# A hybrid decoder layer in split fp32: branch low parts on one engine, output weights staged in twos, and four PSUM banks for the first output tiles

## The chip, the cores and the metric

The kernel runs on one core of one Trainium2 chip. The core has five engines, each with its own list of instructions that it works through in order: PE (TensorE, matrix products, with PEld for its weight loads), DVE (VectorE), ACT (ScalarE), POOL (GpSimd) and SP (SyncE, which here only issues DMAs). The engines wait for one another through semaphores. PE reads its operands from SBUF and writes its products to PSUM. The metric is the device time of one execution in microseconds.

## The reference

One pre-norm decoder layer (DEPTH is 1) with 1024 positions and model width 1024, in fp32:

```python
h = rmsnorm(x, norm_mix)
dq, dk, dv, rq, rk, rv, rg, lx, ly, gates = jnp.split(h @ w_in, splits, axis=-1)
od  = diff_attention(dq, dk, dv, lam)           # then rmsnorm
o_r = silu(rg) * group_norm_heads(retention_chunkwise(q_r, k_r, v_r, log_g))
o_l = rg_lru_branch(lx, ...) * gelu(ly)
g = sigmoid(gates.reshape(bn, s_len, 3, 1024))
merged = (g[:, :, 0] * (od @ w_branch[0]) + g[:, :, 1] * (o_r @ w_branch[1])
          + g[:, :, 2] * (o_l @ w_branch[2]))
x = x + merged @ w_out
x = x + cross_attention(rmsnorm(x, norm_xattn), rmsnorm(mem, norm_mem)) @ xa_wo
x = x + square(relu(rmsnorm(x, norm_mlp) @ mlp_w1)) @ mlp_w2
return rmsnorm(x, norm_final)
```

The change lies at `merged` and at `merged @ w_out`.

## The kernel before

*Split products.* Every fp32 operand of a product is held as two parts: a high part, which ACT makes by a cast (`dst.hi`, L70), and a low part, the rest, which DVE or POOL makes by a subtraction (`dst.lo`, L71; the third argument of `split` chooses the engine). A product is three matmuls: high by high, high by low, low by high (`mm3`, L59 to L61). A 128x512 unit of weights and a 128x1024 piece of an activation block are split in this way before PE can use them.

*The branch products.* The three products `o @ w_branch` are computed transposed, with seven half-size products in place of eight (a Strassen-Winograd scheme). A *pair* is two 128-column strips of a branch's weights. For each of the seven products k of a pair, `product` (L1161) accumulates four `mm3`, twelve matmuls, in one PSUM bank; DVE adds the results into the temporaries `t0` and `t1` (L1182, L1184, L1187), and when an output quarter is complete it calls `emit`. The order of k in a pair is `ORDER = (1, 2, 6, 7, 5, 4, 3)`, in the last two pairs `LAST = (1, 2, 6, 7, 5, 3, 4)`. A branch has four pairs: 0 and 1 run one after the other, 2 and 3 alternate product by product.

*Weights of a pair.* `h_products` makes a list of preparations, `prep(p, k)`, and each product takes the next one from it (`ahead`), so that a unit is prepared some products before its use. `prepare` (L1140) splits the weight unit of (p, k). Low parts of k = 1 and 2 go to DVE; those of the others to the engine that `prep` (L669) passes: POOL for the pairs before number m, which belong to the input projections, and for the branches (p >= m) DVE where k is 6 or 4 and POOL where k is 7, 5 or 3. After k = 2, `left` (L1117) lets DVE make the sums of weight quarters. `pair_load` loads the raw weights into a staging buffer; its L1128 is the DMA.

*Activation blocks.* Seven blocks of 128x(4x512) hold the right operands of a branch. `fill_block` (L787) issues the two DMAs of one block and then splits the block of the call before. The blocks of the next branch are loaded during the last two pairs of the one that runs. Blocks live in two pools of four slots, `slotA` and `slotB`.

*emit* (in `branch`, L819): load the gate tile `sgb` (five buffers), sigmoid on ACT, load the partial sum of the branches before (`pv`), then on DVE `o = x + y` (L828), `o *= sg` (L829), `o += pv` (L831), and a store to DRAM (L833). In the third branch the upper half of the result (n >= 4) is not stored but split straight into the blocks `mT[j][1]` (L835); the lower half is stored and loaded again as `mT[j][0]` by `fill_block` (L867 to L871).

*The end of the third branch.* The weights of the output product, `w_o`, come in eight units of 128x1024; the first four (the left 512 output columns) pass through one staging tile `wst` of 128x(2x512) and are split into two blocks of `slotB`, at k = 7, 5, 3 and 4, by DVE and POOL in turn (L872 to L880). The load of the next unit is issued right behind each split. A last `fill_block()` (L881) splits `mT[0][0]`. The other four units (right columns) are loaded and split by `weight` (L83), low parts on POOL.

*The output product*, `w_out` (L884): for each pair of 128-row tiles and each column half `cb` two PSUM banks of the pool `ps` (which has two in all) accumulate eight `mm3` each. The first half of the rows uses `mT[1]`, the second `mT[0]`. DVE adds the product to the rows of x (L906); for `cb == 1` the row is stored and normed, and its transposes are put off by one step (`later`). The pool `xps` has room for the cross-attention's tiles `tp`, `sc` and `av`; nothing uses `sc` while `w_out` runs.

*What sets the order.* The code above is emitted in program order, and the framework's scheduler turns it into one list per engine at build time. It goes by program order as priority and by its own estimates of when operands and buffers come free, so later work can stand among earlier work where it expects a gap. `after(key, ins)` keeps instructions with the same key in program order: `hdma` the block and `wst` loads, `wdma` the weight loads, `wsplit` the casts of weights. On the chip each list is worked through strictly in that order.

Of the kernel before, what the change touches and what calls it, by code (L numbers as in the profile page):

```python
# [9 lines left out]
F32 = mybir.dt.float32  # L10
# [7 lines left out]
P = 128  # L18
S = 1024
D = 1024  # L20
KT = 8
HB = 512
MEM = 256
# [26 lines left out]
class Kernel:  # L50
# [596 lines left out]
    def h_products(self):  # L647


        nc, v, a = self.nc, self.nc.vector, self.a  # L650
# [17 lines left out]

        def prep(p, k):  # L669
            self.pair_load(p, *pairs[p])  # L670
            self.prepare(k, pairs[p][0], v if p >= m and k in (6, 4) else nc.gpsimd)

            turns = [x for x in (0, m - 2, m + 2, m + 6, m + 10) if x <= p < x + 2]
            q, at = (p + 1, 6) if not turns else (turns[0] + 2, 3 if p > 1 else 4)
            if k == at and p == (turns or [p])[0] and q < len(pairs):
                self.pair_load(q, *pairs[q])
# [135 lines left out]
    def branch(self, order, i, right, bw, sps, nxt):  # L812

        nc, v = self.nc, self.nc.vector
        after, load = (None, None) if nxt is None else self.load_blocks(nxt)
        mT = [[None, None], [None, None]]
        cs = self.bcs[order]

        def emit(n, j, x, y):  # L819
            rows, sl = slice(n * P, (n + 1) * P), slice(j * HB, (j + 1) * HB)  # L820
            sg = bw.tile([P, HB], F32, tag="sg", name="sgb", bufs=5)
            nc.sync.dma_start(sg, self.gsp[i * D + n * P:i * D + (n + 1) * P, sl])
            nc.scalar.activation(sg, sg, AF.Sigmoid)
            if order > 0:
                pv = bw.tile([P, HB], F32, tag="pv", name="pv", bufs=3)
                nc.sync.dma_start(pv, self.acc[order - 1][rows, sl])
            o = bw.tile([P, HB], F32, tag="y", name="y", bufs=4)
            v.tensor_tensor(o, x, y, op=ALU.add)  # L828
            v.tensor_tensor(o, o, sg, op=ALU.mult)  # L829
            if order > 0:  # L830
                v.tensor_tensor(o, o, pv, op=ALU.add)  # L831
            if nxt is not None or n < 4:
                nc.sync.dma_start(self.acc[order][rows, sl], o)  # L833
            else:
                self.split(mT[j][1][:, n % 4, :], o)  # L835

        def run(p, k):
            self.ahead()
            self.product(k, cs[p], right, self.p6(sps), lambda e, j, x, y: emit(2 * p + e, j, x, y))

        for p in range(2):
            for k in self.ORDER:
                run(p, k)

                if (p, k) == (0, 1):
                    next(self.loading)
                elif (p, k) == (0, 2):
                    self.fill_block()
        if nxt is not None:
            for at, k in enumerate(self.ORDER):  # L850
                run(2, k)
                if at > 0:
                    next(load)
                run(3, k)
            self.loading = load
            return after
        w, units = [], 0
        for k in self.LAST:
            run(2, k)
            run(3, k)  # L860

            if k == 1:
                mT[0][1] = self.block(self.slotA)
            elif k == 6:
                mT[1][1] = self.block(self.slotB)
            elif k in (2, 3):
                j = 3 - k  # L867
                mT[j][0] = self.block(self.slotA)
                x = self.acc[2][:, j * HB:(j + 1) * HB].rearrange("(k p) c -> p k c", p=P)
                self.fill_block(mT[j][0], x)  # L870

            if k in (7, 5, 3, 4):  # L872
                if k in (7, 3):
                    w.append(self.block(self.slotB))
                q = units % 2
                self.split(w[-1][:, 2 * q:2 * q + 2, :], wst, (v, nc.gpsimd)[q])
                units += 1
            if k in (1, 7, 5, 3):
                wst = bw.tile([P, 2, HB], F32, tag="wst", name="wst")
                self.after("hdma", nc.sync.dma_start(wst, self.a["w_o"][0, units].rearrange("p (k c) -> p k c", k=2)))  # L880
        self.fill_block()  # L881
        return mT, w

    def w_out(self, half, mT, w, hx, work, psum):  # L884

        nc, a = self.nc, self.a
        for jp in (0, 2):
            xts = []
            for cb in range(2):
                pss = [self.ps.tile([P, HB], F32, tag="mm", name="pso") for _ in range(2)]  # L890

                for kt, e in [(kt, e) for q in range(2) for e in range(2) for kt in range(4 * q, 4 * q + 4)]:
                    s = slice((jp + e) * P, (jp + e + 1) * P)
                    self.mm3(pss[e], mT[1 - half][kt // 4][:, kt % 4, s], w[cb][kt // 2][:, kt % 2, :], kt == 0, kt == KT - 1)
                for e in range(2):
                    j = jp + e
                    rows, back = (slice((4 * n + j) * P, (4 * n + j + 1) * P) for n in (half, 1 - half))
                    if cb == 0:
                        xts.append(work.tile([P, D], F32, tag="xt", name="xt2", bufs=2))
                        (nc.sync if half or jp else nc.scalar).dma_start(xts[e], a["x"][back, :])  # L900
                        if half == 0 and j == 0:
                            self.gx = self.gain(work, 1)
                    xt = xts[e]
                    ps = pss[e]
                    sl = slice(cb * HB, (cb + 1) * HB)
                    nc.vector.tensor_tensor(xt[:, sl], xt[:, sl], ps, op=ALU.add)  # L906
                    if cb == 1:
                        nc.sync.dma_start(self.x2[rows, :], xt)
                        xs = self.norm_rows(xt, self.gx, work)
                        self.later(lambda xs=xs, j=j: self.rows_T(xs, [b[:, :, j * P:(j + 1) * P] for b in hx], psum))  # L910
# [440 lines left out]
    def run(self):  # L1351
        tc, nc, a = self.tc, self.nc, self.a
        pool = lambda name, bufs=1, side="right", **kw: tc.tile_pool(name=name, bufs=bufs, side=side, reuse_waits="tile", **kw)
        self.setup()
        with pool("slotA", bufs=4, side="left") as self.slotA:
            self.n_gates, self.gate_order = 0, [b * 8 + n for b in (1, 0, 2) for n in range(8)]
            with pool("ret") as self.rp, pool("rps", space=PSUM) as self.rps:
                self.retention(pool)
            with pool("att") as self.ap, pool("aps", space=PSUM) as self.aps:
                self.attention()  # L1360
            with pool("slotB", bufs=4) as self.slotB:
                with pool("sps", space=PSUM) as sps:
                    with pool("sp") as self.sp:
                        self.sps = sps
                        for _ in self.hp:
                            pass
                    with pool("bw") as bw:
                        right = self.branch(0, 1, self.right, bw, sps, 0)
                        right = self.branch(1, 0, right, bw, sps, 2)
                        mT, w0 = self.branch(2, 2, right, bw, sps, None)  # L1370
                A, B = self.slotA, self.slotB
                with pool("work") as work:
                    with pool("xps", bufs=2, space=PSUM) as xps:
                        w = [[w0[u // 2][:, u % 2 * 2:u % 2 * 2 + 2, :] for u in range(4)]]
                        w.append([self.weight(a["w_o"][1, u], 2) for u in range(4)])
                        hx = [[self.block(s) for s in (B, A)]]
                        self.w_out(0, mT, w, hx[0], work, xps)
                        hx.append([self.block(s) for s in (A, B)])
                        self.w_out(1, mT, w, hx[1], work, xps)
                        self.mem_slot()  # L1380
                        self.mem_norm(work)
                        g = self.xattn(hx, work, xps)
                    with pool("mps", space=PSUM) as self.mps:
                        self.xa_last(g)
                        self.mlp_in()
                    with pool("m2ps", bufs=6, space=PSUM) as m2ps:
                        self.mlp_out(m2ps)
# [76 lines left out]
```

## Time and profile before

| what | value |
|---|---|
| three runs | 2419.88, 2423.28, 2424.56 us (median 2423.28) |
| the profiled execution, its own time | 2424.15 us |
| its span on the core | 2422.4 us, mean granted PE clock 0.981 |
| busy PE / PEld | 2319.7 / 1913.1 us |
| busy DVE / ACT / POOL | 1888.0 / 1041.4 / 955.9 us |

The three branches run from about 1240 to 1498 us after the span's start, and the output product from 1498 to 1614. A row of the profile's groups names the source line, the engine, the operation and the tiles (out<-in); then the count, the busy time and the mean duration in ns, and the idle time of the engine just before those instructions with what ended most of it. A timeline row begins with the start and the duration in us, and where the engine stood idle before, the idle time and its releaser stand in brackets. `SPq` and `ACTq` are the sequencers that issue DMAs. A row of the windows view gives the stretch and its length, and then for PE, PEld, DVE, ACT and POOL the busy time with the count of instructions, and at the end the granted clock, the DMA share and GB/s. A row of the waits view gives the total, the number of waits and the longest.

### The profile page before, as it was taken

How to read it: one execution, taken by the hardware profiler on the slowest of the kernel's cores; microseconds unless marked ns; L12 is line 12 of the kernel's file. 1: busy time of each engine (PE TensorE's matmuls, PEld its weight loads, DVE VectorE, ACT ScalarE, POOL GpSimd, SP SyncE). 2: the span in 40 equal slices, each digit the busy share in tenths (PEclk: the TensorE clock that was granted, in tenths of full speed). 3: DMA queues.
4: the chain of work that ended last, by engine and by line, in shares of the span. 5: the costliest groups of instructions: out<-in, count | busy, mean ns of one | idle time of the engine just before them, and what ended most of it. 6: DMA issues, size and time to landing. Idle time of an engine off the chain costs nothing. (4 is left out here: it accounts for less than half of the span.)

```text
span 2422.4 us, 31108 instructions
## 1 busy us (share of the span) xinstructions
PE 2319.7 (96%) x11156; PEld 1913.1 (79%) x11156; DVE 1888.0 (78%) x2909; ACT 1041.4 (43%) x1817; POOL 955.9 (39%) x621
## 2 busy tenths in 40 slices
PE   9999999999999998999999988999989999899998
PEld 7888878888887876777887767778768888788886
DVE  7677487878797788798787898344788888788896
ACT  5443355555555543554354444135442222343333
POOL 1122212222215444455431223034155555598863
PEclk9999999999999999999999999999999999999999
DMA  5222122222215354543576687343225443744341
GB/s 173 81 87 70 58 70 60 64 71 70 62 49 180 127 162 162 174 134 136 178 266 240 228 287 239 105 146 119 97 83 183 152 144 135 254 167 166 121 165 70
DMA packets 135994, 335.12 MB, mean 138 GB/s; under 512 B 17040, under 2 KB 27281, under 8 KB 135840
## 3 DMA queue, kind: packets, MB, share of 16 engines
q1 hardware_dynamic: 135264, 331.30, 41.4%
q8 instruction: 89, 1.46, 0.2%
q10 hardware_dynamic: 576, 1.84, 0.2%
q14 instruction: 65, 0.53, 0.1%
HBM read 227.64 MB, written 97.05 MB: 134 GB/s over the span
## 5 line engine op out<-in xcount | busy, mean ns | idle before, releaser
L59 PE MATMUL ps<-block,wu 128*128 128x512 f32 x1428 | 568.6, 398 | 27.2 <-DVE sf L1187 10.4
L61 PE MATMUL ps<-block,wu 128*128 128x512 f32 x1428 | 565.3, 396 | 10.2 <-DVE wu L71 10.2
L60 PE MATMUL ps<-block,wu 128*128 128x512 f32 x1428 | 561.9, 394 | 0.8 <-DVE block L71 0.8
L71 POOL TENSOR_TENSOR wu<-st,wu 128x512 fp32r<-128x512 f32 x144 | 227.3, 1585 | 303.4 <-ACT wu L70 290.4
L59 PEld LDWEIGHTS ps<-block,wu 128*128 128x128 f32 x1428 | 272.4, 191 | 89.0 <-DVE sf L1187 11.3
L61 PEld LDWEIGHTS ps<-block,wu 128*128 128x128 f32 x1428 | 271.2, 190 | 75.1 <-DVE wu L71 13.3
L60 PEld LDWEIGHTS ps<-block,wu 128*128 128x128 f32 x1428 | 271.8, 190 | 61.0 <-DVE block L71 1.3
L70 ACT CAST wu<-st 128x512 fp32r<-128x512 f32 x240 | 141.9, 620 | 210.1 <-DVE st L1117 94.1
L71 POOL TENSOR_TENSOR w<-st,w 128x1024 fp32r<-128x1024 f32 x50 | 124.6, 2501 | 176.7 <-ACT w L70 176.5
L59 PE MATMUL ps<-wu,hu 128*128 128x512 f32 x456 | 179.4, 394 | 8.0 <-ACT wu L70 4.2
L60 PE MATMUL ps<-wu,hu 128*128 128x512 f32 x456 | 178.9, 392 | 0.9 <-POOL wu L71 0.8
L61 PE MATMUL ps<-wu,hu 128*128 128x512 f32 x456 | 178.6, 392 | 0.0
L71 POOL TENSOR_TENSOR wu<-sf,wu 128x512 fp32r<-128x512 f32 x63 | 122.2, 1954 | 131.9 <-ACT wu L70 95.8
L1273 DVE TENSOR_TENSOR acc<-acc,ps 128x512 f32<-128x512 f32 x184 | 118.1, 679 | 19.8 <-PE ps L61 19.4
L71 DVE TENSOR_TENSOR hu<-sth,hu 128x1024 fp32r<-128x1024 f32 x53 | 118.1, 2231 | 14.3 <-ACT hu L70 13.6
L466 ACT ACTIVATE p<-sc,mx 128x256 f32<-128x256 f32 (+7 forms) x128 | 94.8, 742 | 69.9 <-DVE mx L463 50.1
L71 DVE TENSOR_TENSOR wu<-st,wu 128x512 fp32r<-128x512 f32 x96 | 91.1, 960 | 30.9 <-ACT wu L70 30.8
L59 PEld LDWEIGHTS ps<-wu,hu 128*128 128x128 f32 x456 | 86.3, 189 | 28.7 <-ACT wu L70 4.6
L59 PE MATMUL psk<-block,w 128*128 128x512 f32 x256 | 101.6, 397 | 0.0
L60 PEld LDWEIGHTS ps<-wu,hu 128*128 128x128 f32 x456 | 86.3, 189 | 19.3 <-POOL wu L71 1.3
L61 PE MATMUL psk<-block,w 128*128 128x512 f32 x256 | 101.2, 395 | 0.0
L60 PE MATMUL psk<-block,w 128*128 128x512 f32 x256 | 100.8, 394 | 0.0
(383 smaller groups left out, 5627.4 us busy)
## 6 DMA issues: line engine op xcount, KB each, us to landing
sth<-h SPq DMA_DIRECT2D x53, 512.0 KB, 3.2
st<-in_w SPq DMA_DIRECT2D x32, 512.0 KB, 4.2
h<-hab SPq DMA_DIRECT2D x32, 512.0 KB, 2.8
w<-in_w SPq DMA_DIRECT2D x8, 2048.0 KB
block<-oTs SPq DMA_DIRECT2D x24, 512.0 KB, 5.8
sgb<-gsp SPq DMA_DIRECT2D x48, 256.0 KB, 5.3
gsp<-l SPq DMA_DIRECT2D x44, 256.0 KB, 2.8
acc<-y SPq DMA_DIRECT2D x40, 256.0 KB, 2.9
```

What stands on the lines that cost most here:

```text
L59: nc.tensor.matmul(ps, lhsT=lhs.hi, rhs=rhs.hi, start=start, stop=False)
L60: nc.tensor.matmul(ps, lhsT=lhs.hi, rhs=rhs.lo, start=False, stop=False)
L61: nc.tensor.matmul(ps, lhsT=lhs.lo, rhs=rhs.hi, start=False, stop=stop)
L70: ins = self.nc.scalar.copy(dst.hi, src)
L71: self.lo_ins = (lo_engine or self.nc.vector).tensor_tensor(dst.lo, src, f32(dst.hi), op=ALU.subtract)
L466: nc.scalar.activation(p[:, 0:n], sc[:, 0:n], AF.Exp, bias=mx, accum_out=l)
L1273: v.tensor_tensor(acc[k][:, st, :], acc[k][:, st, :], ps, op=ALU.add)
```

## The change

- In the branches all low parts of the weight units are made by DVE; those of the input projections stay as they were.
- `wst` holds two units (128x2048). Units 0 and 1 are loaded at k = 1, both are split at k = 7, and units 2 and 3 are loaded then and split at k = 5. All four low parts are DVE's. To make room, the gate tiles `sgb` have four buffers instead of five.
- The block `mT[1][0]` is split after k = 7, and `mT[0][0]` inside `w_out`, after the fourth output tile's addition.
- The third and fourth tile of the output product (first tile pair, second column half) accumulate in two banks of the tag `sc` of `xps`.
- The low parts of the second four units of `w_o` are made by DVE.

```diff
-            self.prepare(k, pairs[p][0], v if p >= m and k in (6, 4) else nc.gpsimd)
+            self.prepare(k, pairs[p][0], v if p >= m else nc.gpsimd)
...
-            sg = bw.tile([P, HB], F32, tag="sg", name="sgb", bufs=5)
+            sg = bw.tile([P, HB], F32, tag="sg", name="sgb", bufs=4)
...
-            if k in (7, 5, 3, 4):
-                if k in (7, 3):
-                    w.append(self.block(self.slotB))
-                q = units % 2
-                self.split(w[-1][:, 2 * q:2 * q + 2, :], wst, (v, nc.gpsimd)[q])
-                units += 1
-            if k in (1, 7, 5, 3):
-                wst = bw.tile([P, 2, HB], F32, tag="wst", name="wst")
-                self.after("hdma", nc.sync.dma_start(wst, self.a["w_o"][0, units].rearrange("p (k c) -> p k c", k=2)))
-        self.fill_block()
+            if k in (7, 5):
+                w.append(self.block(self.slotB))
+                for q in range(2):
+                    self.split(w[-1][:, 2 * q:2 * q + 2, :], wst[:, q].rearrange("p (k c) -> p k c", k=2))
+            if k in (1, 7):
+                wst = bw.tile([P, 2, D], F32, tag="wst", name="wst")
+                for q in range(2):
+                    self.after("hdma", nc.sync.dma_start(wst[:, q], self.a["w_o"][0, (0 if k == 1 else 2) + q]))
+            if k == 7:
+                self.fill_block()
...
-                pss = [self.ps.tile([P, HB], F32, tag="mm", name="pso") for _ in range(2)]
+
+                if half == 0 and jp == 0 and cb == 1:
+                    pss = [psum.tile([P, 2, MEM], F32, tag="sc", name="pso", bufs=2).rearrange("p a m -> p (a m)") for _ in range(2)]
+                else:
+                    pss = [self.ps.tile([P, HB], F32, tag="mm", name="pso") for _ in range(2)]
...
+                    if half == 0 and j == 1 and cb == 1:
+                        self.fill_block()
...
-                        w.append([self.weight(a["w_o"][1, u], 2) for u in range(4)])
+                        w.append([self.weight(a["w_o"][1, u], 2, lo=nc.vector) for u in range(4)])
```

More of the change, by code (lines that the diff above doesn't have):

```diff
@@ L856, in branch @@
             return after
-        w, units = [], 0
+        w = []
         for k in self.LAST:
```

## The prediction

> **What bounds the kernel now.** I read the page first, then the windows of the stage that the change touches.
>
> ```profile
> span 2422.4 us, 31108 instructions
> PE 2319.7 (96%) x11156; PEld 1913.1 (79%) x11156; DVE 1888.0 (78%) x2909; ACT 1041.4 (43%) x1817; POOL 955.9 (39%) x621
> ...
> 1240.00:1330.00 90.00, 89.23 (x391) 73.01 (x389) 75.58 (x94) 42.43 (x63) 18.66 (x12) 1.00 0.71 241
> 1330.00:1420.00 90.00, 80.59 (x336) 65.20 (x336) 80.61 (x105) 42.20 (x63) 20.24 (x12) 0.94 0.78 257
> 1420.00:1470.00 50.00, 46.61 (x191) 37.14 (x192) 44.13 (x64) 23.03 (x38) 14.18 (x6) 0.93 0.80 277
> 1470.00:1498.00 28.00, 28.00 (x124) 22.95 (x123) 25.44 (x27) 13.21 (x20) 14.59 (x8) 1.00 0.57 188
> 1498.00:1525.00 27.00, 15.65 (x50) 10.99 (x49) 23.75 (x25) 10.18 (x13) 10.79 (x5) 0.68 0.69 237
> ```
>
> PE is the bound, so only what leaves it idle or slow counts. Each window row gives busy time and count of PE, PEld, DVE, ACT and POOL, then the clock. From 1470 to 1498 PE started 124 matmuls in 28.0 us, 0.226 us each; that is its full pace. By it the other rows lack 1.6, 14.1, 6.8 and 15.7 us, 38.2 us in all, and that is the most this stage can give back. PE's own timeline shows where:
>
> ```profile
> 1332.00 0.79 PE L59 MATMUL ps<-block,wu 128*128 128x512 f32 x1 [2.78 <-ACT wu L70]
> 1336.11 0.80 PE L61 MATMUL ps<-block,wu 128*128 128x512 f32 x1 [2.88 <-DVE wu L71]
> 1336.70 0.63 PE L59 MATMUL ps<-block,wu 128*128 128x512 f32 x1
> 1337.13 0.63 PE L60 MATMUL ps<-block,wu 128*128 128x512 f32 x1
> ...
> 1422.22 0.79 PE L59 MATMUL ps<-block,wu 128*128 128x512 f32 x1 [6.75 <-ACT wu L70]
> ...
> 1506.87 0.80 PE L59 MATMUL pso<-block 128*128 128x512 f32 x1 [3.48 <-ACT block L70]
> 1515.89 0.80 PE L59 MATMUL pso<-block 128*128 128x512 f32 x1 [5.66 <-ACT block L70]
> 1518.83 0.80 PE L60 MATMUL pso<-block 128*128 128x512 f32 x1 [2.14 <-POOL block L71]
> ```
>
> There are three places: A (1332, first to second branch), B (1422, second to third) and C (1503 to 1519, third branch to the output product). After a pause the starts stand 0.43 apart (1336.70, 1337.13), half pace. At C the pauses sum to 11.3 of the 15.7 us, and the other 4.4 are that slow restart. What ended B's pause and what ended C's is seen in the other engines' timelines; B's first, then C's:
>
> ```profile
> 1413.60 0.69 DVE L831 TENSOR_TENSOR y<-y,pv 128x512 f32<-128x512 f32 x1
> 1414.32 0.32 SPq L833 DMA_DIRECT2D acc<-y  x1
> 1414.74 0.88 SPq L791 DMA_DIRECT2D block<-oTs  x2
> 1420.60 1.05 ACT L70 CAST block<-block 128x1024 fp32r<-128x1024 f32 x1 [5.99 <-DMA block<-oTs]
> ```
>
> ```profile
> 1491.73 1.06 ACT L70 CAST block<-wst 128x1024 fp32r<-128x1024 f32 x1 [5.41 <-DMA wst<-in_w_o]
> 1495.31 0.33 SPq L880 DMA_DIRECT2D wst<-in_w_o  x1
> 1501.61 0.34 SPq L880 DMA_DIRECT2D wst<-in_w_o  x1
> 1514.27 0.62 ACT L70 CAST block<-y 128x512 fp32r<-128x512 f32 x1 [3.14 <-DVE y L831]
> 1514.80 1.04 ACT L70 CAST block<-wst 128x1024 fp32r<-128x1024 f32 x1
> 1515.92 2.86 POOL L71 TENSOR_TENSOR block<-wst,block 128x1024 fp32r<-128x1024 f32 x1 [2.23 <-ACT block L70]
> 1520.38 0.68 DVE L71 TENSOR_TENSOR block<-y,block 128x512 fp32r<-128x512 f32 x1
> ```
>
> At B a late DVE held SP's store of y, the block's load stood behind that store, ACT waited for the load, and the weight cast that PE needed stood behind ACT's wait. At C two things are late together. The four output-weight units pass through one staging buffer, so the fourth was loaded only at 1501.61. Its cast then stood behind a cast that waited for DVE, and its low part ran on POOL until 1518.78. DVE's list of this stage ends at 1520.38 + 0.68, about 1521.
>
> **The change, part by part.** *Low parts of the branch weights and of the second output weights to VectorE.* The rows are groups of 1240 to 1522, first DVE's, then POOL's; after them DVE's of 1470 to 1522.
>
> ```profile
> L71 DVE TENSOR_TENSOR block<-block 128x1024 fp32r<-128x1024 f32 x39 | 52.3, 1340 | 3.8 <-ACT block L70 3.6
> L829 DVE TENSOR_TENSOR y<-y,sgb 128x512 f32<-128x512 f32 x48 | 47.7, 995 | 1.6 <-ACT sgb L823 1.3
> L71 DVE TENSOR_TENSOR wu<-st,wu 128x512 fp32r<-128x512 f32 x40 | 34.2, 860 | 7.9 <-ACT wu L70 7.9
> L828 DVE TENSOR_TENSOR y<-ps,sf 128x512 f32<-128x512 f32 x48 | 32.8, 685 | 11.3 <-DMA block<-odT 6.0 <-ACT sf L1178 5.4
> L831 DVE TENSOR_TENSOR y<-y,pv 128x512 f32<-128x512 f32 x32 | 27.5, 864 | 0.7 <-DMA pv<-acc 0.5
> ```
>
> ```profile
> L71 POOL TENSOR_TENSOR wu<-sf,wu 128x512 fp32r<-128x512 f32 x18 | 33.0, 1846 | 111.6 <-ACT wu L70 75.7 <-DMA st<-in_w_br 22.4 <-DVE l L693 13.6
> L71 POOL TENSOR_TENSOR wu<-st,wu 128x512 fp32r<-128x512 f32 x18 | 30.0, 1665 | 78.9 <-ACT wu L70 78.9
> ```
>
> ```profile
> L829 DVE TENSOR_TENSOR y<-y,sgb 128x512 f32<-128x512 f32 x8 | 11.4, 1426 | 0.0
> L831 DVE TENSOR_TENSOR y<-y,pv 128x512 f32<-128x512 f32 x8 | 11.1, 1393 | 0.1
> L71 DVE TENSOR_TENSOR block<-y,block 128x512 fp32r<-128x512 f32 x8 | 8.2, 1030 | 2.0 <-ACT block L70 1.9
> ...
> L71 DVE TENSOR_TENSOR block<-wst,block 128x1024 fp32r<-128x1024 f32 x2 | 2.4, 1211 | 0.0
> ```
>
> One 128x512 subtraction that reads PSUM takes 685 ns, and so does the quickest with both inputs in SBUF (0.69 at 1413.60). Yet the groups with two SBUF inputs average 995, 860 and 864. I take the excess as time in which POOL's instruction held them up: 48 x 0.305 + 40 x 0.17 + 32 x 0.174 + 39 x 0.129 (against 1211) = 14.6 + 6.8 + 5.6 + 5.0 = 32.0 us. The change gives DVE 36 more at 0.69 (24.8 us) and, at C, six wide ones at 1.21 (four second output weights, two staged units; 7.3 us). So DVE takes on 32.1 and sheds 32.0 us: over the whole stage its load stays what it is, and POOL falls idle. At A and B I therefore expect little: the work that had been fastest on DVE (A's and B's backlogs of y) is no longer interrupted, but three more subtractions a pair stand in its list. From below a loss is possible (the first rival); from above, half of the 20.9 us of A and B. I take 2 us, since the excess lies where both engines run and a DVE that is x earlier brings B's block load x earlier.
>
> At C the balance is better. The excess there is 8 x 0.736 + 8 x 0.703 + 8 x 0.34 = 14.2 us. POOL's 8 + 5 instructions in the last two window rows are twelve (one lies in both): six wide ones and six of branch weights. DVE takes on the six of branch weights (4.1) and the six wide ones (7.3), and gives the two low parts of the merged block mT[0][0] (2.4) to a later stage. 14.2 + 2.4 - 11.4 = 5.2 us: its list would end near 1516 rather than 1521, and without the four second output weights (4.8), which are needed last, near 1511.
>
> *Two units staged at once.* Units 0 and 1 are loaded together; 2 and 3 are issued when the splits of 0 and 1 are done. Before, the split of unit 1 had its cast at 1491.73, and two loads and splits still followed. Now one load of both follows: issued about 1493 or earlier, landed after the 5.41 us that ACT waited for such a load, 1499, cast 2 x 1.05, ready for DVE by 1501. It no longer needs the round that began at 1501.61. SP issues four DMAs as before; the second of each two goes ahead of the gates' loads, 0.3 us of issue. What is late next is DVE. PE reached the fourth-unit half of its first pair at 1506.87 - 3.48 = 1503.4, and can go on there between 1503.4 (DVE takes what PE needs first) and 1511.1 (DVE takes all the y before it). A pause of 7.7 us with its share of the slow restart (4.4 x 7.7 / 11.3 = 3.0) leaves 5.0 of the 15.7 us as gain; no pause leaves 15.7. I take 10.5, about the middle: the list is written in due order, but the planner decides.
>
> On that restart the Trainium skill, "TensorE: Matmul & The Clock Gate", section "HAM oscillation — how this bites in real kernels", says that only pauses above some 3.4 us throttle the array. Here A's 2.78 and 2.88 us were already followed by half pace, so I keep the restart in; by the page, a pause of 3 us left at C would cost 1.2 us less, and the sum would be 1.2 lower.
>
> *The block mT[0][0] later.* Two casts and two subtractions go behind the first tile pair, where DVE has room (it is needed only by the second half, some 40 us on). I cost it at nothing; without that cover it costs its 2.4.
>
> *Four banks for the first four tiles.*
>
> ```profile
> 1519.37 0.82 ACTq L900 DMA_DIRECT2D xt<-in_x  x2
> ...
> 1523.03 0.69 DVE L906 TENSOR_TENSOR xt<-xt,pso 128x512 f32<-128x512 f32 x1 [1.97 <-DMA xt<-in_x]
> ```
>
> The third tile's bank was free only after the addition of 1523.03, which waited for a load that ACT issued behind its last cast of the branch. PE did not lose by it, since it was later still. Earlier products would meet it; with four banks they don't. Alone worth 0; if it failed, C would keep up to the 3.7 us from issue to addition.
>
> *Four buffers for the gates instead of five.*
>
> ```profile
> SPq L822 <- DVE y L829: 21.4, 8, 7.9
> ```
>
> This queue entry already waits 8 times out of 48 for a buffer. One fewer makes more such waits, and all of SP's list stands behind them. Between 0 and 5 us (two of the longest waits, a third of them reaching PE); I take 0.5.
>
> **The sum.** 10.5 + 2 - 0.5 = 12 us. The profiled execution took 2424.15 us (span 2422.4, 1.75 around it), 0.87 above the median of 2423.28; 2424.15 - 12 gives 2412.
>
> **The rivals.**
> 1. *VectorE's list becomes the wait (slower).* The POOL rows show 75.7 + 78.9 = 154.6 us of waiting for ACT's casts, harmless because POOL had nothing else. On DVE the same subtraction stands in front of the y of the next tiles; SP's stores wait for those, the block loads for the stores. DVE already runs 80.61 of 90 us in the second branch. It decides once DVE's idle time over 1240 to 1525 (285 less 249.5 busy in the five rows, 35.5) grows beyond some 40. Price: B's 6.75 twice more, 13.5, C's gain cut to 5: 2424 + 8.5, about 2432. Against it: the four other low parts of each pair do this already and waited only 7.9 us. The Trainium skill's "TensorE: Matmul & The Clock Gate" (Architectural detail) calls VectorE's queue a strict FIFO; by that rule this is the outcome wherever a cast is late.
> 2. *C's wait only changes its name.* The planner puts the second output weights (4.8 us) ahead of the y that PE needs: going on at 1511.1 + 4.8 = 1515.9 instead of 1518.8 gains 3, with A and B 4.5: 2419.5, no change that can be measured. For it: POOL's casts of these weights already ran among the y.
> 3. *Everything closes.* C gives all 15.7 and A and B half of 20.9: 2424 - 26 = 2398. For it: one late DVE links all three. Against: A and B waited on DMA landings, which nothing here shortens.
> 4. *It doesn't do what it says.* The planner leaves the last weight loads where they were, and the time stays at 2424.
>
> **How the numbers follow.** Forecast 0.54, rivals 0.14, 0.12, 0.12 and 0.08. A change within 0.2% (4.8 us) cannot be told from none. Faster: 0.54 + 0.12 + 0.04 of the second rival = 0.70; same: 0.08 + 0.08 = 0.16; slower 0.14. The range 2398 to 2424 takes in rivals 2, 3 and 4 and leaves out the first and a little of the third.
>
> **What would show it.** In the new profile: no POOL subtraction between 1240 and 1520; L829 back at 690 ns; PE's pauses at C below 8 us in sum, the last no longer ended by POOL; the two late staged loads issued before 1496; A and B within 2 us of now; DVE's list of the branch done by 1516. It is wrong if DVE's waits for ACT's casts grow past 15 us, or if B's pause grows.

## The result and the profile after

| | time before | time changed | ratio, 95% interval |
|---|---|---|---|
| measured | 2423.92 us, median of 4 | 2398.85 us (2397.63 to 2401.78), median of 4 | 0.9905 (0.9888 to 0.9923) |

The kernel is faster by 0.95%, some 23 us by the ratio. That lies inside the predicted range of 2398 to 2424, but only 0.85 us above its lower end, which is less than executions of one kernel differ by; 2412 was forecast. The profiled execution took 2399.68 us. First its page and its windows, with the same columns as before:

```profile
span 2397.8 us, 31053 instructions
PE 2312.2 (96%) x11156; PEld 1908.5 (80%) x11156; DVE 1869.8 (78%) x2951; ACT 1040.5 (43%) x1817; POOL 884.1 (37%) x579
```

```profile
1240.00:1330.00 90.00, 90.00 (x395) 73.95 (x394) 76.08 (x112) 46.00 (x68) 0.00 (x0) 1.00 0.75 253
1330.00:1420.00 90.00, 85.34 (x368) 68.44 (x367) 85.56 (x127) 47.37 (x72) 0.00 (x0) 1.00 0.84 285
1420.00:1470.00 50.00, 48.39 (x209) 38.66 (x208) 48.01 (x77) 25.40 (x42) 0.00 (x0) 1.00 0.84 283
1470.00:1498.00 28.00, 28.00 (x124) 22.94 (x124) 26.77 (x39) 13.18 (x18) 0.00 (x0) 1.00 0.60 197
1498.00:1525.00 27.00, 25.31 (x115) 20.62 (x114) 12.73 (x17) 4.58 (x8) 1.11 (x2) 1.00 0.58 195
```

POOL is idle through the branches. At PE's full pace of 0.226 us a matmul the rows now lack 0.7, 6.8, 2.8, 0 and 1.0 us, 11.3 in all, where they lacked 38.2. The clock stands at 1.00 in every row, so this execution has no slow restart either (a second profile of the changed kernel has one, with 0.94 in the last row). These are the pauses that PE has left at A and B; at C it has none.

```profile
1333.01 0.50 PE L61 MATMUL ps<-block,wu 128*128 128x512 f32 x1 [0.57 <-DVE wu L71]
1353.46 0.50 PE L59 MATMUL ps<-block,wu 128*128 128x512 f32 x1 [0.93 <-ACT wu L70]
1415.10 0.50 PE L61 MATMUL ps<-block,wu 128*128 128x512 f32 x1 [3.06 <-DVE wu L71]
1424.15 0.50 PE L61 MATMUL ps<-block,wu 128*128 128x512 f32 x1 [0.53 <-DVE wu L71]
1436.26 0.50 PE L59 MATMUL ps<-block,wu 128*128 128x512 f32 x1 [1.02 <-ACT wu L70]
```

DVE's groups between 1240 and 1522 us:

```profile
L71 DVE TENSOR_TENSOR wu<-st,wu 128x512 fp32r<-128x512 f32 x58 | 39.2, 684 | 7.4 <-ACT wu L70 7.4
L829 DVE TENSOR_TENSOR y<-y,sgb 128x512 f32<-128x512 f32 x48 | 32.7, 684 | 2.3 <-ACT sgb L823 2.3
L828 DVE TENSOR_TENSOR y<-ps,sf 128x512 f32<-128x512 f32 x48 | 32.7, 684 | 1.0 <-PE ps L61 1.0
L831 DVE TENSOR_TENSOR y<-y,pv 128x512 f32<-128x512 f32 x32 | 21.8, 683 | 0.0
```

Operations with two SBUF inputs take the same 684 ns as those that read PSUM; the means of 995, 864 and 860 are gone. The timeline of C, where the two late units are loaded together, cast and split:

```profile
1471.99 2.04 SPq L878 DMA_DIRECT2D wst<-in_w_o  x2
1478.99 1.99 ACT L70 CAST block<-wst 128x1024 fp32r<-128x1024 f32 x2
1482.48 1.22 DVE L71 TENSOR_TENSOR block<-wst,block 128x1024 fp32r<-128x1024 f32 x1
```

The last low part is done by 1483.7, 35 us earlier than before. To compare kernels I use two stretches that the rows of a tile give: from the start of DVE's first `y` (L828) to that of PE's first `pso` (the branches), and from there to the start of PE's last `pso` (the output product). Before, then changed; in each row the first and last start stand behind the durations:

```profile
L828 DVE TENSOR_TENSOR y<-ps,sf x48: 676/685/695, 1256.0 to 1511.4; 128x512 f32<-128x512 f32 x48
...
L59 PE MATMUL pso<-block x64: 388/394/796, 1497.7 to 1596.2; 128*128 128x512 f32 x64
...
L61 PE MATMUL pso<-w,block x64: 388/389/398, 1525.2 to 1607.6; 128*128 128x512 f32 x64
```

```profile
L828 DVE TENSOR_TENSOR y<-ps,sf x48: 676/684/694, 1258.3 to 1492.9; 128x512 f32<-128x512 f32 x48
...
L59 PE MATMUL pso<-block x64: 388/394/486, 1488.6 to 1572.3; 128*128 128x512 f32 x64
...
L61 PE MATMUL pso<-w,block x64: 388/389/398, 1500.0 to 1583.6; 128*128 128x512 f32 x64
```

The branches went from 241.7 to 230.3 us, the output product from 109.9 to 95.0: 11.4 and 14.9 us. The experiments ask which edit gave which.

### The profile page after: what moved, and what is told of

Read it like the earlier page. It is cut to its first block, busy times and chain, and to the rows that moved or that the text cites. A ratio compares the mean times of both kernels' runs of the same rounds, so it can differ in the third digit from the quotient of the medians.

```text
span 2397.8 us, 31053 instructions
## 1 busy us (share of the span) xinstructions
PE 2312.2 (96%) x11156; PEld 1908.5 (80%) x11156; DVE 1869.8 (78%) x2951; ACT 1040.5 (43%) x1817; POOL 884.1 (37%) x579
## 5 line engine op out<-in xcount | busy, mean ns | idle before, releaser
L71 POOL TENSOR_TENSOR wu<-st,wu 128x512 fp32r<-128x512 f32 x126 | 200.3, 1596 | 224.1 <-ACT wu L70 204.5
L71 POOL TENSOR_TENSOR w<-st,w 128x1024 fp32r<-128x1024 f32 x46 | 115.0, 2509 | 169.3 <-ACT w L70 169.1
L97 POOL TENSOR_TENSOR rs<-rs,mhalf 128x1 f32<-128x1 f32 x26 | 14.6, 562 | 412.1 <-DVE rs L96 412.1
L71 DVE TENSOR_TENSOR wu<-st,wu 128x512 fp32r<-128x512 f32 x114 | 97.5, 866 | 32.7 <-ACT wu L70 32.7
```

What stands on the lines that cost most here:

```text
L71: self.lo_ins = (lo_engine or self.nc.vector).tensor_tensor(dst.lo, src, f32(dst.hi), op=ALU.subtract)
L97: self.nc.gpsimd.tensor_tensor(dst, dst, self.mhalf[:, : dst.shape[-1]], op=ALU.pow)
```

## The experiments

Each line of the table is one profile for the two stretches and several executions for the time; the ratio is to the kernel before on the same chip. Executions of one kernel differ by some us (the kernel before: 2415.5 to 2428.3 on one chip), so differences of 2 us between kernels say nothing. The two stretches don't add up to a difference in time either: the two MLP stages behind them, which no edit touches, took between 639 and 647 us together in these profiles, from one matmul to the same matmul.

| kernel | branches us | output product us | median us | ratio, 95% interval |
|---|---|---|---|---|
| before | 241.7 | 109.9 | 2423.92 | |
| before, profiled again | 241.4 | 109.5 | 2424.76 (one) | |
| changed | 230.3 | 95.0 | 2398.85 | 0.9905 (0.9888 to 0.9923) |
| changed, again | 231.3 | 97.1 | 2399.20 | 0.9905 (0.9885 to 0.9925) |
| branch low parts only | 228.8 | 104.1 | 2401.36 | 0.9918 (0.9896 to 0.9940) |
| all but branch low parts | 238.8 | 96.2 | 2403.86 | 0.9930 (0.9910 to 0.9950) |
| changed, with idle POOL work | 241.2 | 97.1 | 2406.05 | 0.9939 (0.9915 to 0.9962) |
| four gate buffers only | 238.0 | 106.8 | 2420.66 | 0.9996 (0.9982 to 1.0011) |
| changed, two banks | 229.4 | 102.1 | 2404.40 | 0.9923 (0.9906 to 0.9939) |
| changed, second weights on POOL | 237.3 | 93.8 | 2397.66 | 0.9899 (0.9878 to 0.9919) |
| changed, no deferral | 228.7 | 94.6 | 2396.67 | 0.9901 (0.9883 to 0.9919) |
| changed, staged singly | 230.7 | 94.7 | 2393.23 | 0.9881 (0.9865 to 0.9896) |
| the same again | 231.1 | 93.8 | 2391.48 | 0.9879 (0.9864 to 0.9894) |
| the same, five gate buffers | 227.7 | 94.4 | 2391.18 | 0.9879 (0.9864 to 0.9894) |

### Branch low parts alone, and all but them

To the kernel before:

```diff
-            self.prepare(k, pairs[p][0], v if p >= m and k in (6, 4) else nc.gpsimd)
+            self.prepare(k, pairs[p][0], v if p >= m else nc.gpsimd)
```

> The kernel before with one edit: all low parts of the branch weight units on DVE; staging, banks, gate buffers and the second output weights as before. Theory P (DVE was held up by POOL's subtractions): the two SBUF-input groups fall to about 690 ns up to 1470, the losses of the branch transitions fall from 22 us to about 10, and C keeps most of its pauses since the output weights still come one at a time; time about 12 to 14 below before, near 2411. Theory S (the gain is the new staging and what the scheduler then put elsewhere): A and B stay, 2422 to 2426. Theory F (the moved subtractions wait in DVE's list for ACT's casts, and only the other edits pay for it): slower than before, above 2428.

To the changed kernel, the same line the other way round:

> The changed kernel with one edit undone: low parts of k = 7, 5, 3 in the branches back on POOL. Theory P: A and B lose about 20 us again as before, C stays closed or nearly (pauses under 4 us); time 2399 + 10 to 13, near 2411. Theory S: A and B stay as in the changed kernel, within 4 us of 2399.

PE's pauses with the low parts alone:

```profile
1340.73 0.50 PE L61 MATMUL ps<-block,wu 128*128 128x512 f32 x1 [1.09 <-DVE wu L71]
1411.36 0.51 PE L61 MATMUL ps<-block,wu 128*128 128x512 f32 x1 [1.64 <-DVE wu L71]
...
1497.23 0.64 PE L59 MATMUL pso<-block 128*128 128x512 f32 x1 [4.33 <-ACT block L70]
1499.65 0.79 PE L60 MATMUL pso<-block 128*128 128x512 f32 x1 [1.79 <-POOL block L71]
```

And with everything else:

```profile
1416.46 0.79 PE L59 MATMUL ps<-block,wu 128*128 128x512 f32 x1 [6.46 <-ACT wu L70]
1421.09 0.79 PE L61 MATMUL ps<-block,wu 128*128 128x512 f32 x1 [2.98 <-DVE wu L71]
...
1501.91 0.50 PE L59 MATMUL pso<-block 128*128 128x512 f32 x1 [1.82 <-ACT block L70]
```

The low parts all but close B and keep a smaller C; the rest all but closes C and keeps B. Theory F falls, and so does theory S for B. A is short in both: its longest pause is 1.09 us with the low parts alone and 1.28 us with the rest, where the kernel before has 2.78 and 2.88. In the two stretches the low parts give 12.9 + 5.8 us and the rest 2.9 + 13.7; added they would be 35.3, together they give 26.3. They share 9 us, half of it in the branches (15.8 added, 11.4 together), where either closes A, and half in the output product (19.5 added, 14.9 together).

### POOL work that nobody waits for

```diff
+            if p >= m + 2 and k in (7, 5, 3):
+                hi = f32(pairs[p][0]["u", k].hi.rearrange("p k c -> p (k c)"))
+                for s in (slice(0, 256), slice(256, 512)):
+                    nc.gpsimd.tensor_tensor(self.idle, hi[:, s], self.idle, op=ALU.subtract)
```

> The changed kernel with POOL work added that nobody waits for: for each branch unit with k = 7, 5, 3 of ten of the twelve pairs POOL subtracts a scratch tile from the high part in two halves of 128x256, 60 instructions. Theory P in its pure form (interference alone): DVE's two-input groups rise by 20 to 30 us in sum again, DVE falls behind, and A and B lose 6 to 10 us again; time 2405 to 2410. If the gain at A and B came from the units being ready sooner and the raw-weight loads no longer waiting for POOL, and not from DVE being held up: the DVE groups may rise, but the time stays within 3 us of 2399.

POOL's group, then three of DVE's (L832 and L833 are what was L828 and L829), two windows, then PE's pauses:

```profile
L675 POOL TENSOR_TENSOR idle<-wu,idle 128x256 f32<-128x256 f32 x60 | 87.9, 1465 | 136.1 <-ACT wu L70 132.1
```

```profile
L833 DVE TENSOR_TENSOR y<-y,sgb 128x512 f32<-128x512 f32 x48 | 36.7, 766 | 1.7 <-ACT sgb L827 1.5
L832 DVE TENSOR_TENSOR y<-ps,sf 128x512 f32<-128x512 f32 x48 | 32.5, 678 | 0.0
...
L71 DVE TENSOR_TENSOR wu<-sf,wu 128x512 fp32r<-128x512 f32 x24 | 22.2, 927 | 0.2 <-ACT wu L70 0.2
```

```profile
1330.00:1420.00 90.00, 80.59 (x343) 63.91 (x342) 86.72 (x122) 43.92 (x66) 42.65 (x26) 0.97 0.81 270
1420.00:1470.00 50.00, 49.51 (x210) 39.32 (x210) 47.51 (x70) 21.84 (x39) 21.38 (x15) 0.98 0.79 266
```

```profile
1414.13 0.50 PE L59 MATMUL ps<-block,wu 128*128 128x512 f32 x1 [2.29 <-ACT wu L70]
1418.75 0.80 PE L61 MATMUL ps<-block,wu 128*128 128x512 f32 x1 [3.89 <-DVE wu L71]
...
1495.14 0.51 PE L61 MATMUL ps<-block,wu 128*128 128x512 f32 x1 [3.67 <-DVE wu L71]
```

DVE's operations with two SBUF inputs became longer again (766 and 927 for 684), those that read PSUM did not (678). In sum DVE's groups rose by some 15 us, less than the 20 to 30 expected. No wait of DVE, ACT or PE for this POOL work appears in the profile, so it is not late data: the interference alone costs time, as theory P said.

How much of the change it explains is less clear. The branches took 241.2 us, as in the kernel before, but not for the same pauses. A stays closed (no pause above 0.98 us). In the two rows that hold A and B (1330 to 1470), PE lacks 12.5 and 2.5 us at 0.226 a matmul: 15.0, against 20.9 in the kernel before, 18.4 with all but the branch low parts and 9.6 in the changed kernel, so about half of that gain is gone. The rest of the 241.2 is the pause of 3.67 us at 1495, which neither of the two has; POOL's last idle subtraction was over at 1479.3, and from there to the pause every operation of DVE has its undisturbed length, so this delay seems to be carried on in DVE's list for 15 us. And this POOL work (87.9 us) is more than the 63.0 us that the change took away. The other half of A's and B's gain may come from the other order of the lists, or from raw weights that no longer wait for POOL; no run settles it. The time is 7 to 8 us longer, not the 13 of the two stretches, mostly since the MLP stages took 4.3 us less in this execution than in the changed kernel's.

### Four gate buffers alone, and the kernel before again

```diff
-            sg = bw.tile([P, HB], F32, tag="sg", name="sgb", bufs=5)
+            sg = bw.tile([P, HB], F32, tag="sg", name="sgb", bufs=4)
```

> The kernel before with four gate buffers instead of five and nothing else. By the prediction's term 0 to 5 us slower, 0.5 taken; by the rival that buffers set the order of SP's list: more than 5 us either way.

> The kernel before once more, for a second profile of it. Its executions spread from 2415 to 2429 us, the profiled one took 2424.15. If the spread lies at the branch transitions: a faster execution shows A's pauses (2.78 and 2.88 us) gone or B's and C's shorter; if the pauses are fixed by the lists, they stand where they were, within 1 us.

With four buffers, then the kernel before in its second profile:

```profile
1349.72 0.50 PE L61 MATMUL ps<-block,wu 128*128 128x512 f32 x1 [1.33 <-DVE wu L71]
1415.33 0.79 PE L59 MATMUL ps<-block,wu 128*128 128x512 f32 x1 [6.47 <-ACT wu L70]
...
1509.28 0.80 PE L59 MATMUL pso<-block 128*128 128x512 f32 x1 [6.54 <-ACT block L70]
```

```profile
1337.09 0.80 PE L61 MATMUL ps<-block,wu 128*128 128x512 f32 x1 [3.36 <-DVE wu L71]
1424.29 0.80 PE L59 MATMUL ps<-block,wu 128*128 128x512 f32 x1 [7.87 <-ACT wu L70]
...
1520.56 0.80 PE L60 MATMUL pso<-block 128*128 128x512 f32 x1 [2.15 <-POOL block L71]
```

The kernel before has its three places in both profiles, though this execution took 2424.76 us like the first; what the faster ones look like stays unknown. With four buffers A shrinks in the one profile there is (an execution of 2415.88 us, among the fastest of ten), as it did in the run with all but the branch low parts, which has four buffers too. So A may not need the low parts at all; one profile of each doesn't show it. The median over ten executions is that of the kernel before: four buffers cost nothing that can be measured.

### Two banks, no deferral, second weights on POOL

```diff
-                if half == 0 and jp == 0 and cb == 1:
-                    pss = [psum.tile([P, 2, MEM], F32, tag="sc", ...) for _ in range(2)]
-                else:
-                    pss = [self.ps.tile([P, HB], F32, tag="mm", name="pso") for _ in range(2)]
+                pss = [self.ps.tile([P, HB], F32, tag="mm", name="pso") for _ in range(2)]
```

> The changed kernel with the third and fourth output tile back in the two banks of the pool that the first two use. By the prediction's cost of the cover: up to 3.7 us slower, since the products now arrive before the load of x that the additions wait for. If the banks are worth nothing: within 1.5 us of the changed kernel.

PE, then ACT's queue, then DVE in that kernel:

```profile
1504.88 0.79 PE L59 MATMUL pso<-w,block 128*128 128x512 f32 x1 [6.66 <-DVE xt L906]
```

```profile
1497.30 0.82 ACTq L900 DMA_DIRECT2D xt<-in_x  x2
```

```profile
1504.14 0.69 DVE L906 TENSOR_TENSOR xt<-xt,pso 128x512 f32<-128x512 f32 x1 [2.33 <-DMA xt<-in_x]
```

PE waits 6.66 us for the bank that the first addition frees, and that addition waits for a load issued at 1497.30. The output product takes 102.1 instead of 95.0 to 97.1, and the median is 5 us more, though the two intervals overlap. The banks keep what the other edits gain; what they are worth alone no run shows.

```diff
+        self.fill_block()
         return mT, w
...
-                    if half == 0 and j == 1 and cb == 1:
-                        self.fill_block()
```

> The changed kernel with the split of the block mT[0][0] at the end of the branch instead of inside the output product. The prediction costed the deferral at nothing while it is covered and at 2.4 us without cover: with it undone 0 to 2.5 us slower than the changed kernel (ratio 0.9905 to 0.9915); if ACT's two casts and DVE's two subtractions hold PE's second tile pair, up to 5 us.

Without the deferral the time is 0.9901 of before and the output product 94.6 us: no difference from the changed kernel. No gain of it can be measured.

```diff
-                        w.append([self.weight(a["w_o"][1, u], 2, lo=nc.vector) for u in range(4)])
+                        w.append([self.weight(a["w_o"][1, u], 2) for u in range(4)])
```

> The changed kernel with the low parts of the second four output-weight units back on POOL. If POOL's wide subtractions hold up DVE at C (theory P): DVE's y groups after 1470 rise again by 1 to 2 us an overlap, a pause of 2 to 5 us at C, time 2401 to 2404. If they only share the work: within 1.5 us, perhaps a little faster, since DVE has 4.8 us less to do.

POOL, DVE and PE with the second weights back on POOL:

```profile
1480.86 6.62 POOL L71 TENSOR_TENSOR w<-st,w 128x1024 fp32r<-128x1024 f32 x2 [5.39 <-DVE block L71]
```

```profile
1482.68 2.60 DVE L71 TENSOR_TENSOR block<-y,block 128x512 fp32r<-128x512 f32 x1 [0.18 <-ACT block L70]
1485.20 2.83 DVE L71 TENSOR_TENSOR wu<-st,wu 128x512 fp32r<-128x512 f32 x1
```

```profile
1488.09 0.79 PE L61 MATMUL ps<-block,wu 128*128 128x512 f32 x1 [4.83 <-DVE wu L71]
```

Two wide subtractions on POOL stretch two of DVE's from 0.69 to 2.6 and 2.8 us, and PE waits 4.83 us for the second. The branches take 237.3 us; yet the median is not higher than the changed kernel's. In the profiled execution the MLP stages took 3.2 us less than in the changed kernel's, and the branches began 3.6 us earlier; so the verdict on the time is "no difference shown".

### Staged singly

```diff
-            if k in (7, 5):
-                w.append(self.block(self.slotB))
-                for q in range(2):
-                    self.split(w[-1][:, 2 * q:2 * q + 2, :], wst[:, q].rearrange("p (k c) -> p k c", k=2))
-            if k in (1, 7):
-                wst = bw.tile([P, 2, D], F32, tag="wst", name="wst")
...
+            if k in (7, 5, 3, 4):
+                if k in (7, 3):
+                    w.append(self.block(self.slotB))
+                q = units % 2
+                self.split(w[-1][:, 2 * q:2 * q + 2, :], wst)
+                units += 1
+            if k in (1, 7, 5, 3):
+                wst = bw.tile([P, 2, HB], F32, tag="wst", name="wst")
...
```

> The changed kernel with the staging undone: one unit of the output weights in the staging tile at a time, split at k = 7, 5, 3 and 4, all low parts still on DVE, four gate buffers, banks and deferral as changed. If C's wait was the serial round of load, cast and low part (the prediction's reading): a pause of 4 to 8 us returns at C, time 2403 to 2407. If C's wait was DVE being held up by POOL's subtractions: C stays closed, time within 2 us of the changed kernel.

> The changed kernel with the output weights staged one unit at a time, again, in more rounds: if staging in twos costs time, the ratio to the kernel before stays at 0.988 and below the changed kernel's 0.9905; if the difference of 6 us was chance between executions, it comes out at 0.990.

> The same with five gate buffers, as before the change (there is room for them without the double staging tile). If four buffers make SP wait and this reaches PE (the prediction's 0.5 us, at most 5): 0.5 to 3 us faster than with four. If the number only shifts the lists: within 3 us either way.

The staging tile of the first of these kernels (loads, then low parts):

```profile
L879 SPq DMA_DIRECT2D wst<-in_w_o x4: 327/340/422, 1432.9 to 1481.9; - x4
...
L71 DVE TENSOR_TENSOR block<-wst,block x4: 1220/1226/1227, 1466.1 to 1492.0; 128x1024 fp32r<-128x1024 f32 x4
```

The last unit is loaded at 1481.9 and its low part begins at 1492.0, where the changed kernel began it at 1482.48. It still comes in time: the output product takes 94.7 and 93.8 us. Staging in twos gave nothing. With one unit at a time the time is even lower, 0.988 in three measurements, though the intervals just overlap the changed kernel's. The branches and the output product are equally long, so that gain lies elsewhere. The windows of the two MLP stages, of the changed kernel and of the second single one:

```profile
1743.40:2067.90 324.50, 313.30 (x1362) 255.14 (x1360) 269.41 (x328) 84.12 (x146) 176.50 (x112) 0.99 0.43 148
2067.90:2387.50 319.60, 313.71 (x1363) 257.69 (x1364) 274.75 (x298) 121.42 (x147) 234.90 (x96) 0.98 0.43 152
```

```profile
1740.30:2062.30 322.00, 314.75 (x1362) 256.47 (x1360) 267.24 (x328) 83.90 (x145) 176.81 (x112) 0.98 0.43 149
2062.30:2379.80 317.50, 311.71 (x1363) 256.81 (x1364) 274.75 (x298) 121.51 (x147) 234.10 (x96) 0.99 0.42 153
```

The same matmuls in the same order take 2.5 and 2.1 us less, in code that no edit touches. It is not the staging: from one matmul to the same matmul, kernels staged in twos have such short stages too (322.6 us for the first with the second weights on POOL, 316.9 for the second with idle POOL work, against 325.6 and 318.7 in the changed kernel). Why is not settled. Staged singly, with four or five gate buffers, is the best version measured, 2391 to 2393 us.

## Why the prediction was right in sign and half in size

*What bounds the kernel.* Right. The 38.2 us that PE lacked between 1240 and 1525 were what could be had; 26.9 of them came back (38.2 - 11.3), and the time fell by about as much.

*Low parts at A and B: 2 us taken, 11.4 measured in the branches.* The size failed, at the step "over the whole stage its load stays what it is ... I therefore expect little". The balance itself held: DVE was busy for 225.8 us and PE started 1042 matmuls in the four windows up to 1498, 0.217 us each; afterwards it was 236.4 us and 1096 matmuls, 0.216. (The sum of the excess left out two smaller groups, `block<-y` and `wu<-sf`, some 4.5 us; they don't change the reading.) But the balance does not set the pauses. With idle POOL work DVE's load is 0.230 us a matmul, and the branches take as long as in the kernel before with its 0.217. Interference from POOL can account for about half of the gain in the rows of A and B, as that run shows; how it gets to PE is argued and not measured. At B it was not an operation held on the spot: from 1401 us to B's pause POOL does nothing in the kernel before, and every operation of DVE there has its undisturbed length. The delay is older, and the prediction had seen what can carry it on: DVE's y, SP's store, the block's load, ACT's cast. Its upper bound, half of A's and B's 20.9 us, was closer to the truth than the value taken.

*Output product: 10.5 taken, 14.9 measured,* inside the bounds of 5.0 and 15.7, near the end at which DVE takes what PE needs first. The direction was right, but half the reason was wrong. Of the step "two things are late together" the staging needed no cure of its own: with all low parts on DVE the single staging tile is in time. What made C, then, was low parts made by POOL, the two staged ones and those beside which DVE's operations ran longer; no run parts these two.

*Four banks.* "Alone worth 0; if it failed, C would keep up to the 3.7 us": the pause was 6.66 us and the time 5 us more. The cover was rightly named and undersized: from the issue of the load to the addition it was 3.7 us in the kernel before (1519.37 to 1523.03) and 6.8 in this run (1497.30 to 1504.14).

*Deferral, four gate buffers.* 0 and 0.5 us predicted, neither measurable.

*The slow restart.* By the Trainium skill ("TensorE: Matmul & The Clock Gate", "HAM oscillation — how this bites in real kernels") only pauses above about 3.4 us should throttle. The traces don't agree. Half pace followed pauses of 2.88 us in the kernel before, 2.57 with two banks and, 0.6 us behind it, 1.64 with the low parts alone; full pace followed 3.06 us in the changed kernel and 3.17 with the second weights on POOL. So the size of a pause alone doesn't decide it. The same page of the Trainium skill ("What's actually happening") calls the window free-running; then the place of a pause in the window would count too, but half pace after 1.64 us stays unexplained. The prediction was right to keep the restart in; its "1.2 lower" by the page holds for the time, while the gain would be higher.

*The rivals.* The first (DVE's list becomes the wait) did not happen: DVE's waits for ACT's casts of weights are 7.4 + 1.5 us in the changed kernel against 7.9 + 3.4 before, where its sign was growth past 15. The second did not happen either: no pause at C. The third came closest, at 2398 predicted and 2398.85 measured: C closed whole, and A and B gave half. Its reason, that one late DVE links all three, fits the runs, though none of them shows the whole chain. It had been given 0.12, because A and B waited on DMA landings; those DMAs were themselves issued late, behind stores of a late DVE.

*The range and the signs.* The number is right by luck in part: 12 us were forecast and 25 came, and it lies in the range because that reached down to the third rival's price. Of the signs all came true but one: A and B did not stay within 2 us.

## What to carry to other kernels

Where one engine's work makes another's operations longer, as POOL's subtractions did here, price a subtraction on the idle engine not only by its own time but also by what it does to the operations of the busy one that it overlaps, and ask who waits for that engine's list further on. A balance of busy times that comes out even doesn't mean that nothing changes. Test the parts of a change singly: here the low parts alone bring most of the gain and the banks keep some 5 us of it, while no gain came from the double staging that looked like the cure for C. And before a difference in time is put down to an edit, look at the stages that the edit doesn't touch.

## What the runs showed of the hardware that was not expected

- A 128x512 subtraction of DVE with two SBUF inputs takes 684 ns alone, and 2.6 to 2.8 us beside wide POOL subtractions of 128x1024; operations that read PSUM stay at means of 677 to 689 ns in all profiles, with POOL busy or idle.
- A POOL subtraction of half the width, 128x256, took 1465 ns on average beside a busy DVE (median 1076, longest 4560), not much less than the 1665 and 1846 ns (medians 1730 and 1742) of the 128x512 ones in the kernel before.
- Stages with identical lists of work, 300 us behind the edit, differed by 2 to 2.5 us between kernels, and executions of the kernel before by up to 12.8 us on one chip.
- PE fell to half pace 0.6 us behind a pause of 1.64 us in one kernel, and went on at full pace after 3.17 us in another.
